# An encoder trunk's attention rebuilt: projections as Strassen groups summed in PSUM, heads' work in slots between products

## The chip, the core and the metric

One core of a Trainium2 chip runs the whole program. The metric is the device time of one execution in microseconds (us). Engines are named as the profile names them: PE is TensorE (matrix products and transposes), PEld its weight loads, DVE the vector engine, ACT the scalar engine, POOL the GpSimd engine, SP the engine that issues the DMA transfers of this kernel. PSUM is the memory into which PE writes its results, eight banks of 512 fp32 numbers in each of 128 partitions; SBUF is the working memory of all engines.

## What is computed

Two layers over a sequence of 1,024 rows of width 1,024. Layer 0 is attention with two families of heads, layer 1 a gated recurrence; each layer ends with a SwiGLU block, and every block is wrapped in two RMS norms. Everything is fp32. The change touches the attention of layer 0:

```python
def attention_mixer(h, w_in, rel_bias, w_out):
    proj = h @ w_in                       # 1024 x 3072
    part_a, part_b = proj[..., :3 * A_W], proj[..., 3 * A_W:]
    qa, ka, va = [t.reshape(b, s, 8, 64) for t in jnp.split(part_a, 3, axis=-1)]
    qs, ks, vs = [t.reshape(b, s, 8, 64) for t in jnp.split(part_b, 3, axis=-1)]
    out_a = chunked_relpos_attention(qa, ka, va, rel_bias)
    out_b = stick_breaking_attention(qs, ks, vs)
    return jnp.concatenate([out_a, out_b], axis=-1) @ w_out

# A, per head: softmax(q k^T / 8 + bias[clipped distance]) v over the own chunk of 64 rows and the 8 before it
# B, per head and block of 128 queries, z = q k^T / 8, keys strictly before the query:
        log_beta = jax.nn.log_sigmoid(z)
        log_1m_beta = jnp.where(causal, jax.nn.log_sigmoid(-z), 0.0)
        after = lax.cumsum(log_1m_beta, axis=3, reverse=True) - log_1m_beta
        w = jnp.where(causal, jnp.exp(log_beta + after), 0.0)
        o = einsum('bhqk,bkhd->bqhd', w, v)
```

A weight of a B head is thus the difference of two neighbouring products of (1 - sigmoid), taken from the query backwards.

## The kernel before

**Precision.** A big product of fp32 operands is made of three matmuls: each operand is split into hi, a copy rounded to the type fp32r, and lo, the rest, and hi·hi, hi·lo and lo·hi are summed in PSUM. `split` (L136 load, L143 hi on ACT, L144 lo on DVE) does this for 128x1024 numbers of weights, in a pool "main" that is open for the whole program (three raw buffers, eight for hi and lo). Transposes and the value products are plain fp32 matmuls.

**Hidden.** `pre_norm` makes the normalized rows of a tile of 128 (L164 squares on ACT, L167 and L168 POOL, L191 scaling on DVE), transposes them in eight 128x128 blocks on PE (L197), and `HiddenT.take` writes hi (L57, ACT) and lo (L58, DVE) of the transposed hidden hT.

**Heads.** Sixteen heads are taken in pairs: pairs 0 to 3 are A heads, 4 to 7 B heads, in the order 4, 5, 6, 7, 0, 1, 2, 3. For two pairs at a time the values are projected (L248 to L250, 24 matmuls of 256 columns for a tile of 128 rows and 4 heads), and copied out of PSUM by DVE (L253). `project` computes q and k of a pair, transposed (`proj_T`, L154 to L156, 512 columns), and lays for each head three operands: qs holds hi of q in 64 partitions and lo in the other 64, k1 and k2 hold hi and lo of k twice. A block of scores is then two matmuls 128 deep for each head and up to 512 keys:

```python
nc.tensor.matmul(sc, q, k1[:, ks], start=True, stop=False)
nc.tensor.matmul(sc, q, k2[:, ks], start=False, stop=True)
```

(L321, L322). `attend` goes over the eight tiles of 128 queries of a pair. An A head takes up to five blocks of 128 keys: bias and minimum on DVE (L325, L332), exponential with its sum on ACT (L333), division on DVE and POOL (L335, L336). A B head takes all blocks up to its own: sigmoid on ACT (L329), the mask on POOL (L338), a running product over the keys on DVE (L341), and the difference of neighbours (L344, DVE). Then for each four blocks of 128x128, PE transposes the weights (L354), ACT or DVE copies them to SBUF (L358, L360), and PE multiplies them with the values (L363: head 0 in the left 64 columns of the array, head 1 in the right). After four tiles ACT copies the output (L369) and SP stores it to DRAM (L370).

**Order.** The code names no order of engines. The framework's scheduler, with a timeline of its own, moves instructions past each other where their data and buffers allow it: the projections of the next pair (L154 to L156, L248 to L250) stand between the scores, transposes and values of the present one, and the loads and splits of the output weights (`out_product`, first load raw_5617) stand ahead of the last pairs' work. PSUM holds two banks for projections, one for outputs, three for scores, two for transposes.

After the attention, `out_product` loads the heads' outputs back (L415) and multiplies them by the output weights (L422 and following), with the pairs in the order of their making.

Of the kernel before, what the change touches and what calls it, by code (L numbers as in the profile page):

```python
# [8 lines left out]
F32 = mybir.dt.float32  # L9
F32R = mybir.dt.float32r  # L10
# [5 lines left out]
P = 128  # L16
# [8 lines left out]
BIG = 1e30  # L25

# [71 lines left out]

class Trunk:
# [4 lines left out]
    def __init__(self, ctx, tc, io):  # L104
# [3 lines left out]
        self.main = ctx.enter_context(tc.tile_pool(name="main", bufs=1))  # L108
# [113 lines left out]
    def attention(self, x_src, w_in, bias_t, o_dst, hT):  # L222
        nc, tc = self.nc, self.tc
        with ExitStack() as ctx:
            ap = ctx.enter_context(tc.tile_pool(name="att", bufs=1, reuse_waits="tile"))
            prp = ctx.enter_context(tc.tile_pool(name="attproj", bufs=1, space=PSUM, reuse_waits="tile"))
            pp = ctx.enter_context(tc.tile_pool(name="attp", bufs=1, space=PSUM, reuse_waits="tile"))

            def w_cols(c0, n):
                return w_in[:, c0:c0 + n].rearrange("(k p) c -> p k c", p=P)  # L230

            vbase = [1024, 1280, 2560, 2816]

            def v_weights(grp):
                wv = w_cols(vbase[grp], 256)
                return [self.split(wv[:, 4 * j:4 * j + 4, :], 4, 256) for j in range(2)]

            def v_tile(grp, w, vt, t2):
                ps = prp.tile([P, 512], F32, tag="proj", bufs=2, name=self.uid("psv"))
                for tt in range(2):  # L240
                    t = 2 * t2 + tt
                    hh, hl = hT.half[t // 4]
                    tok = slice((t % 4) * P, (t % 4) * P + P)
                    o = ps[:, tt * 256:(tt + 1) * 256]
                    for kt in range(KT):
                        wh, wl = w[kt // 4]
                        k4 = kt % 4
                        nc.tensor.matmul(o, hh[:, kt, tok], wh[:, k4, :], start=kt == 0, stop=False)  # L248
                        nc.tensor.matmul(o, hh[:, kt, tok], wl[:, k4, :], start=False, stop=False)
                        nc.tensor.matmul(o, hl[:, kt, tok], wh[:, k4, :], start=False, stop=kt == KT - 1)  # L250
                psv = ps.rearrange("p (a h b) -> p a h b", a=2, h=2)
                for h in range(2):
                    nc.vector.tensor_copy(vt[h][:, 2 * t2:2 * t2 + 2, :], psv[:, :, h, :])  # L253

            def v_alloc():
                return [ap.tile([P, NT, P], F32, tag="v", bufs=3, name=self.uid("v")) for _ in range(2)]

            def project(p):
                qb, kb = (p * P, 512 + p * P) if p < 4 else (1536 + (p - 4) * P, 2048 + (p - 4) * P)
                st = [[ap.tile([P, S], F32R, tag="st", bufs=12, name=self.uid("st"))  # L260
                       for _ in range(3)] for _ in range(2)]
                for which, c0 in ((0, qb), (1, kb)):
                    w = self.split(w_cols(c0, P), KT, P)
                    for half in range(2):
                        ps = prp.tile([P, 512], F32, tag="proj", bufs=2, name=self.uid("psq"))
                        self.proj_T(ps, w, slice(0, P), hT, half)
                        cs = slice(half * HALF, (half + 1) * HALF)
                        for h in range(2):
                            own, oth = (slice(0, 64), slice(64, P)) if h == 0 else (slice(64, P), slice(0, 64))
                            qs, k1, k2 = st[h]  # L270
# [675 lines left out]
```

## Time and profile before

| | before |
|---|---|
| median of 3 runs | 2258.68 us (2257.41 to 2261.26) |
| the profiled execution | 2262.01 us |
| its span | 2260.2 us |
| mean granted clock of PE | 0.993 |
| instructions | 30583 |
| PE busy in the span | 2201.2 us, 97% |
| PE's first transpose of the attention (L197) | 7.8 us |
| PE's first matmul of the output product (L422) | 518.46 us |

The profile is of one execution, and its own time stands beside its span in the table. In its rows an operation is written by engine, line, the names of what it writes and reads (out<-in), and its shape as partitions x elements. "busy" is time in which an engine executes; a wait is the idle time ahead of an instruction, put down to the one that released it. Matmuls overlap, so their price is better read from the distance of their starts than from their durations.

### The profile page before, as it was taken

The page shows a single profiled execution, that of the slowest core. Times are in us where ns is not written, and L with a number is a line of the kernel's source. Part 1 is how long each engine was busy: PE and PEld are TensorE (multiplying, and loading weights), DVE is VectorE, ACT ScalarE, POOL GpSimd, SP SyncE. Part 2 cuts the span into 40 slices and gives each one's busy share as a digit, 9 for nine tenths or more (in the row PEclk, how much of TensorE's full clock was granted, in tenths as well). Part 3 has the DMA queues.
Part 4 walks back from the last instruction along what each step waited for, and adds up shares of the span by engine and source line. Part 5 has one row for each costly group of instructions (what it writes and reads, how often), then busy time and mean ns, then how long its engine had stood idle before and what let it go on. Part 6 is the DMA issues. An engine that isn't in the chain of part 4 may idle for free. (4 is left out here: it accounts for less than half of the span.)

```text
span 2260.2 us, 30583 instructions
## 1 busy us (share of the span) xinstructions
PE 2201.2 (97%) x11136; PEld 1802.0 (80%) x11136; DVE 1551.9 (69%) x2514; ACT 1149.1 (51%) x2132; POOL 168.3 (7%) x370
## 2 busy tenths in 40 slices
PE   7999999999999999999999999999999999999997
PEld 6887888877678888888887777887788888888875
DVE  5676765464677767675866787536777767668665
ACT  4544455464665454532446567527755444424443
POOL 2111212131100000000001100001100000000010
PEclk9999999999999999999999999999999999999998
DMA  4101011124623333334558511358233333327466
GB/s 161 52 20 52 20 48 41 59 97 132 230 83 104 114 115 108 102 118 175 187 148 251 155 56 41 94 175 269 76 125 108 100 115 104 107 98 274 126 205 196
DMA packets 187271, 273.63 MB, mean 121 GB/s; under 512 B 13936, under 2 KB 115312, under 8 KB 187120
## 3 DMA queue, kind: packets, MB, share of 16 engines
q1 hardware_dynamic: 186480, 269.58, 38.0%
q10 hardware_dynamic: 640, 2.10, 0.3%
q8 instruction: 87, 1.43, 0.3%
q14 instruction: 64, 0.52, 0.1%
HBM read 206.09 MB, written 65.54 MB: 120 GB/s over the span
## 5 line engine op out<-in xcount | busy, mean ns | idle before, releaser
L509 PE MATMUL ps<-hS,q 128*128 128x512 f32 (+1 forms) x1288 | 490.9, 382 | 3.1 <-ACT hS L95 3.1
L510 PE MATMUL ps<-hS,q 128*128 128x512 f32 (+1 forms) x1288 | 490.9, 381 | 0.0
L511 PE MATMUL ps<-hS,q 128*128 128x512 f32 (+1 forms) x1288 | 489.9, 381 | 0.0
L490 DVE TENSOR_TENSOR q<-raw,q 128x512 fp32r<-128x512 f32 x308 | 204.7, 686 | 179.2 <-ACT q L489 178.7
L509 PEld LDWEIGHTS ps<-hS,q 128*128 128x128 f32 x1288 | 243.3, 189 | 50.2 <-ACT hS L95 3.9
L510 PEld LDWEIGHTS ps<-hS,q 128*128 128x128 f32 x1288 | 243.9, 189 | 46.7 <-DVE hS L88 0.4
L511 PEld LDWEIGHTS ps<-hS,q 128*128 128x128 f32 x1288 | 244.0, 189 | 45.8
L489 ACT CAST q<-raw 128x512 fp32r<-128x512 f32 x308 | 177.8, 616 | 168.8 <-DVE raw L498 130.4
L590 PE MATMUL ps<-o,o 128*128 128x512 f32 x616 | 240.9, 392 | 0.9 <-DVE o L585 0.8
L591 PE MATMUL ps<-o,o 128*128 128x512 f32 x616 | 238.2, 391 | 0.7 <-DVE o L701 0.7
L589 PE MATMUL ps<-o,o 128*128 128x512 f32 x616 | 221.1, 393 | 9.0 <-ACT o L700 5.5
L584 ACT CAST o<-raw 128x512 fp32r<-128x512 f32 x206 | 123.6, 620 | 193.8 <-PE ps L591 56.0
L478 ACT ACTIVATE raw<-raw,gcol 128x256 f32<-128x256 f32 x352 | 150.2, 498 | 139.0 <-DMA raw<-in_ffn_w_up_dram 71.8
L585 DVE TENSOR_TENSOR o<-raw,o 128x512 fp32r<-128x512 f32 x206 | 137.9, 688 | 66.4 <-ACT o L584 65.6
L589 PEld LDWEIGHTS ps<-o,o 128*128 128x128 f32 x616 | 115.7, 188 | 37.2 <-ACT o L700 7.7
L144 DVE TENSOR_TENSOR wlo<-raw,whi 128x1024 fp32r<-128x1024 f32 x76 | 93.4, 1230 | 66.0 <-ACT whi L143 65.1
L590 PEld LDWEIGHTS ps<-o,o 128*128 128x128 f32 x616 | 116.2, 189 | 26.6 <-DVE o L585 2.9
L591 PEld LDWEIGHTS ps<-o,o 128*128 128x128 f32 x616 | 116.1, 188 | 25.5 <-DVE o L701 1.6
L167 POOL TENSOR_SCALAR rs<-ss 128x1 f32<-128x1 f32 x64 | 31.8, 496 | 1270.2 <-ACT junk L164 1171.0
L143 ACT CAST whi<-raw 128x1024 fp32r<-128x1024 f32 x76 | 79.8, 1052 | 58.5 <-PE ps L155 24.7
L358 ACT COPY pt<-tr 128x512 f32<-128x512 f32 (+1 forms) x128 | 65.5, 527 | 78.5 <-PE tr L354 78.0
L154 PE MATMUL psq<-hT,whi 128*128 128x512 f32 x256 | 101.2, 395 | 1.1 <-DVE v L253 1.1
(185 smaller groups left out, 4237.6 us busy)
## 6 DMA issues: line engine op xcount, KB each, us to landing
raw<-in_ffn_w_down_dram SPq DMA_DIRECT2D x96, 256.0 KB, 4.6
raw<-in_ffn_w_gate_dram SPq DMA_DIRECT2D x44, 512.0 KB, 4.1
raw<-in_ffn_w_up_dram SPq DMA_DIRECT2D x44, 512.0 KB, 4.1
gS<-c SPq DMA_DIRECT2D x88, 256.0 KB, 3.6
raw<-gS SPq DMA_DIRECT2D x88, 256.0 KB, 3.0
gA<-c SPq DMA_DIRECT2D x66, 256.0 KB, 3.4
raw<-in_attn_w_in_dram SPq DMA_DIRECT2D x24, 512.0 KB, 3.9
raw<-in_attn_w_out_dram SPq DMA_DIRECT2D x24, 512.0 KB, 4.3
```

The source lines that it names most:

```text
L154: nc.tensor.matmul(ps, wh[:, kt, cols], hh[:, kt, :], start=kt == 0, stop=False)
L478: nc.scalar.activation(raw[:, i], raw[:, i], AF.Copy, scale=gain[:, 4 * k + i:4 * k + i + 1])
L489: self.last = nc.scalar.copy(t[:, 0], src).ins
L490: nc.vector.tensor_tensor(t[:, 1], src, t[:, 0].bitcast(F32), op=ALU.subtract)
L509: nc.tensor.matmul(ps, a[:, 0, kt, :], bh, start=kt == 0, stop=False)
L510: nc.tensor.matmul(ps, a[:, 0, kt, :], bl, start=False, stop=False)
L511: nc.tensor.matmul(ps, a[:, 1, kt, :], bh, start=False, stop=kt == 3)
L584: nc.scalar.copy(t[:, 0], src)
L585: tt(t[:, 1], src, t[:, 0].bitcast(F32), op=ALU.subtract)
L589: nc.tensor.matmul(ps, a[0], b[:, 0], start=first, stop=False)
L590: nc.tensor.matmul(ps, a[0], b[:, 1], start=False, stop=False)
L591: nc.tensor.matmul(ps, a[1], b[:, 0], start=False, stop=last)
```

## The change

The attention is written anew, and what surrounds it is adapted. Behind the attention the program stays as it was, with two exceptions: the order of pairs in the output product is 0 to 7, and the pool "main" is opened when the attention's pools have been closed, where before it was open from the start.

**Hidden in quadrants.** `HiddenH` holds the hidden as seven operands of a Strassen-Winograd product with hi and lo, in three tiles b0, b1, b2: the two halves of the sequence by the two halves of the width are four blocks, and the seven are these and their sums and differences. Tiles of rows come in the order 0, 4, 1, 5, 2, 6, 3, 7, so that a tile and the one 512 rows behind it can be combined. Behind each tile's transposes the A heads' values are projected from the same operands (24 matmuls of 512 columns) and stored to DRAM.

**Groups and products.** The other 2,560 columns (q and k of eight pairs, the B heads' values) are ten groups of 256 columns. A group is seven products, each 12 matmuls of 512 columns (three for each of four blocks of 128 of the contraction), where the direct way takes eight. Sums of products that share a term go on in the same PSUM bank (`first=False`); the others are added by ACT and DVE as they leave it. q and k go to DRAM and are loaded back for each pair. Values of B heads are differenced along the sequence, transposed back by PE, and stored, so that the running products are used as they are and L344's difference of weights is not made; one column of values is added with the output.

**Scores** are plain fp32 matmuls 64 deep: head 0 in partitions 0 to 63, head 1 in 64 to 127, into two PSUM banks that the next instructions read together. `turn` transposes up to 8 blocks into a double bank, which ACT copies to one buffer pt; the value matmuls of a tile come at the next slot, by `flush`.

**Order.** Each PE job is chained behind the one before (`run`, by issue_after). A slot is the scores of one tile with the transposes of the tile before it, or one of the two where both double banks are needed for one of them. After each product a credit grows by 1.35, up to 2.7; a slot costs 1, and is taken if the groups that its pair needs were ended three products ago. What is left when the products are through follows without any between. PSUM now holds two banks x, one yz, one for outputs, and two double banks "ct" that scores and transposes share.

```diff
+class HiddenH:
+    def take(self, t, ps, pool):
...
+        if t < 4:
+            f = self.f[t] = new("f", 2)
+            for q in range(2):
+                split(b0[0][:, q, :, cols], b0[1][:, q, :, cols], ps[q])
+                cast(f[:, q], ps[q])
+            return lambda z, kt: b0[z][:, kt // 4, kt % 4, cols]
+        b12, b22 = ps
+        f, e = self.f[t - 4], new("e", 1)
+        own = pool.tile([P, 2, 4, P], F32R, tag="own", bufs=1, name=self.uid("own"))
+        cast(e[:, 1], b12)
+        sub(f[:, 0], b12, f[:, 0])
+        split(own[:, 0], own[:, 1], b12)
+        split(b1[0][:, 0, :, cols], b1[1][:, 0, :, cols], b22)
+        sub(e[:, 1], b22, e[:, 1])
+        sub(e[:, 0], b22, f[:, 0])
+        sub(f[:, 1], f[:, 1], e[:, 0])
+        for src, i in ((e, slice(1, 3)), (f, slice(0, 4, 3))):
+            split(b2[0][:, i, :, cols], b2[1][:, i, :, cols], src)
...
-    def attention(self, x_src, w_in, bias_t, o_dst, hT):
+    def attention(self, x_src, w_in, w_v, bias_t, o_dst):
...
+            def run(jobs):
+
+                with tc.issue_after(state["after"]) if state["after"] else nullcontext():
+                    for job in jobs:
+                        state["after"] = job().ins
...
+            order = [0, 1, 2, 3, 8, 4, 5, 9, 6, 7]
...
+            def product(ps, i, first):
...
+                for kt in range(4):
+                    bh, bl = hS.op(i, 0, kt, FULL), hS.op(i, 1, kt, FULL)
+                    for x, y in ((a[:, 0, kt, :], bh), (a[:, 0, kt, :], bl), (a[:, 1, kt, :], bh)):
+                        jobs.append(lambda x=x, y=y, s=first and not jobs, e=kt == 3 and x is not y: nc.tensor.matmul(
+                            ps, x, y, start=s, stop=e, skip_group_check=True))
+                run(jobs)
...
+            def group(g):
...
+                x = bank("x", 2)
+                product(x, 0, True)
+                s1 = tmp()
+                nc.scalar.activation(s1, x, AF.Copy, scale=scale)
+                yield
...
+                product(x, 4, False)
+                u2 = tmp()
+                nc.scalar.copy(u2, x)
+                yield
...
+            def scores(p, i):
...
+                    held["k"] = cp.tile([P, S], F32, tag="k", bufs=1, name=self.uid("k"))
+                    nc.sync.dma_start(held["k"], qk[p][1])
...
+                if i % 4 == 0:
+                    held["q"] = cp.tile([P, 512], F32, tag="q", bufs=1, name=self.uid("q"))
...
+                sc = [pair_bank()[:, :, :w] for _ in range(n_c)]
+                run([lambda c=c, h=h: nc.tensor.matmul(
+                    sc[c][:, h], q[rows[h], i % 4 * P:i % 4 * P + P], k[rows[h], k0 * P + c * w:k0 * P + c * w + w],
+                    start=True, stop=True) for c in range(n_c) for h in range(2)])
...
+            for g in order:
+                for _ in group(g):
+                    unit += 1
+                    credit = min(credit + 1.35, 2.7)
+                    while credit >= 1 and at < len(slots):
+                        p = slots[at][0]
+                        need = [p] if p < 4 else [p, 8 + (p - 4) // 2]
+                        if not all(x in ready and ready[x] + 3 <= unit for x in need):
+                            break
+                        slot()
+                        at += 1
+                        credit -= 1
...
+            while at < len(slots):
+                slot()
+                at += 1
+            flush()
...
+            (nc.scalar.copy if n % 2 else nc.vector.tensor_copy)(vb, o)
...
-        with pool("h0", "right") as hp:
-            self.attention(x, io["attn_w_in"], io["bias_t"], oT, HiddenT(self, hp))
+        self.attention(x, io["attn_w_in"], io["attn_w_v"], io["bias_t"], oT)
+        self.main = ctx.enter_context(tc.tile_pool(name="main", bufs=1, reuse_waits="tile"))
...
-                                 hS, [4, 5, 6, 7, 0, 1, 2, 3])
+                                 hS, list(range(KT)))
```

**The instructions at three places.** Rows give line, operation, out<-in, shape, and xN where N of them follow each other. Lines are those of each kernel's own text; the changed text is longer, so that equal code has a higher line.

First, DVE at the start, where the hidden is made. Before, a tile costs two subtractions of hT, and the copies of values (v) stand among them:

```order
L58 TENSOR_TENSOR hT_100<-pst_244,hT_99 128x4x128
L253 COPY v_112<-psv_186 128x256
L253 COPY v_113<-psv_186 128x256
L58 TENSOR_TENSOR hT_100<-pst_249,hT_99 128x4x128
L144 TENSOR_TENSOR wlo_589<-raw_586,whi_588 128x1024
L58 TENSOR_TENSOR hT_100<-pst_265,hT_99 128x4x128
```

In the change (ct is the double bank that the transposes wrote, hS, own, e and f are hidden operands, x the rows, vb the values of a tile whose 24 matmuls PE has to end first):

```order
L615 SCALAR_TENSOR_TENSOR x_391<-x_391,rs_394,g_135 128x1024
L125 TENSOR_TENSOR hS_129<-e_237,hS_128 128x8x128
L125 TENSOR_TENSOR hS_129<-f_185,hS_128 128x2x4x128
L626 COPY vb_281<-ps_304 128x512
L125 TENSOR_TENSOR f_297<-ct_340,f_297 128x512
L615 SCALAR_TENSOR_TENSOR x_443<-x_443,rs_446,g_135 128x1024
L125 TENSOR_TENSOR hS_125<-ct_400,hS_124 128x4x128
L125 TENSOR_TENSOR own_350<-ct_340,own_350 128x512
```

The subtractions of the next pair of tiles (ct_340, ct_400), which their value matmuls need, now stand behind the copy vb_281.

Second, PE in the middle. Before, with pairs 4 and 5, the scheduler mixes values, transposes, scores (st) and projections of 256 columns one by one:

```order
L249 MATMUL psv_1705<-wlo_1649,hT_99 128x256
L250 MATMUL psv_1705<-whi_1648,hT_100 128x256
L363 MATMUL pso_808<-pt_1054,v_112 64x128 x4
L354 MATMUL tr_1243<-ident,pr_1221 128x128
L354 MATMUL tr_1243<-ident,pr_1232 128x128
L321 MATMUL sc_1295<-st_1082,st_1081 128x384
L322 MATMUL sc_1295<-st_1083,st_1081 128x384
L363 MATMUL pso_808<-pt_1065,v_112 64x128 x4
```

In the change, with the first tiles of pair 0, two slots stand between two products:

```order
L358 MATMUL ps_883<-hS_128,q_739 128x512
L516 MATMUL ps_901<-pt_878,v_899 64x128 x2
L459 MATMUL ct_907<-k_832,q_844 128x384 x2
L499 MATMUL ct_923<-ident,pr_862 128x128 x4
L516 MATMUL ps_901<-pt_922,v_899 64x128 x4
L459 MATMUL ct_935<-k_832,q_844 128x512 x2
L499 MATMUL ct_951<-ident,pr_906 128x128 x6
L358 MATMUL ps_775<-hS_128,q_755 128x512
```

The values from pt_922 stand next behind the scores that follow the transposes ct_923, whose copy pt_922 is; no product lies between.

Third, the end of the attention. Before, on SP, the output weights (raw) stand among and ahead of the last stores of the attention (L370):

```order
L136 DMA raw_5797<-in_attn_w_out_dram 128x1024
L289 DMA bias_5191<-in_bias_t_dram 128x640
L415 DMA act_5735<-oT_73 128x384
L415 DMA act_5765<-oT_74 128x384
L415 DMA act_5795<-oT_75 128x384
L370 DMA oT_75<-ob_5041 128x512
L370 DMA oT_76<-ob_5335 128x512
L370 DMA oT_76<-ob_5583 128x512
```

In the change the first of these weights comes behind the last store (L524):

```order
L510 DMA v_4288<-vn_121 128x1024
L524 DMA oT_76<-ob_4116 128x512
L455 DMA q_4343<-qk_0_116 128x512
L524 DMA oT_77<-ob_4291 128x512
L524 DMA oT_77<-ob_4410 128x512
L189 DMA raw_4587<-in_attn_w_out_dram 128x1024
```

On PE the change ends the attention with the last two tiles of pair 7, no product between them, and the output product (L650) follows:

```order
L459 MATMUL ct_4467<-k_4259,q_4343 128x512 x2
L459 MATMUL ct_4468<-k_4259,q_4343 128x512 x2
L499 MATMUL ct_4481<-ident,pr_4422 128x128 x6
L499 MATMUL ct_4489<-ident,pr_4422 128x128 x8
L516 MATMUL ps_4409<-pt_4480,v_4288 64x128 x14
L499 MATMUL ct_4515<-ident,pr_4466 128x128 x8
L499 MATMUL ct_4525<-ident,pr_4466 128x128 x8
L516 MATMUL ps_4409<-pt_4514,v_4288 64x128 x16
L650 MATMUL ps_4579<-whi_4589,ah_4593 128x512
```

Before, these rows were blocks of four transposes and four values each, as in the second place, with the first matmul of the output product (L422) right behind the last of them.

More of the change, by code (lines that the diff above doesn't have):

```diff
@@ L25 @@
 BIG = 1e30
+FULL = slice(0, 512)
 def rows(t, x):
@@ new lines, in attention @@
+            hS = HiddenH(self, hp)
+            with self.pool("rows") as sp:
+                self.rows_in(ap, sp, x_src, w_v, va, hS, bank, pair_bank, operand)
+            cp = ctx.enter_context(self.pool("core"))
+            state = {"after": None}
+            def run(jobs):
[3 more added lines that the diff above has]
+            order = [0, 1, 2, 3, 8, 4, 5, 9, 6, 7]
```

426 lines of the change are left out of this document (264 added, 162 removed).

## Prediction

> **What bounds the kernel now.** I read the page first, then the busy time by stage, then what TensorE (PE) itself waited for in the stage that the change touches.
>
> ```profile
> span 2260.2 us, 30583 instructions
> PE 2201.2 (97%) x11136; PEld 1802.0 (80%) x11136; DVE 1551.9 (69%) x2514; ACT 1149.1 (51%) x2132; POOL 168.3 (7%) x370
> 7.80:60.00 52.20, 43.62 (x283) 40.93 (x284) 30.77 (x38) 23.85 (x38) 14.11 (x20) 0.93 0.45 148
> 60.00:480.00 420.00, 420.00 (x2973) 350.51 (x2972) 271.25 (x490) 212.48 (x428) 70.30 (x186) 1.00 0.13 40
> 480.00:518.50 38.50, 35.28 (x316) 25.32 (x314) 24.88 (x96) 25.76 (x62) 15.34 (x25) 1.00 0.34 116
> ```
>
> The last three lines are stretches of the span: length, then busy time (instructions) of PE, PEld, DVE, ACT and POOL, granted clock, DMA. The attention is the stretch from PE's first transpose at 7.8 to 518.5 us, where its last value matmul hands over to the output product. In its middle PE is busy without a gap for 420 us while DVE is busy 65% and ACT 51%. The next view, PE's own waits up to 520 us, says the same (waited for, total us, times, longest).
>
> ```profile
> PE pst L197 <- DVE h L191: 7.8, 1, 7.8
> PE psv L250 <- DVE hT L58: 3.5, 2, 2.9
> PE pst L197 <- DVE hT L58: 2.6, 1, 2.6
> PE pso L363 <- ACT pt L358: 2.3, 3, 1.4
> PE psv L248 <- ACT hT L57: 1.5, 2, 1.2
> PE psq L154 <- DVE v L253: 1.1, 1, 1.1
> PE sc L321 <- DVE mn L325: 0.8, 1, 0.8
> ```
>
> After the start, PE waited 11.8 us (the last six lines). So of 518.5 - 7.8 = 510.7 us, **499 us are PE work**. The old order is as full as an order can be: the change can gain only by giving PE less to do, and everything it leaves uncovered is new.
>
> **PE work after the change.** The busy time of a matmul overlaps the next one's, so prices are taken from starts in PE's timeline (start, busy, line, tiles, count).
>
> ```profile
> 168.16 0.39 PE L322 MATMUL sc<-st,st 128*128 128x512 f32 x1
> 168.39 0.39 PE L155 MATMUL psq<-hT,whi 128*128 128x512 f32 x1
> 168.71 0.44 PE L363 MATMUL pso<-pt,v 128*64 128x128 f32 x4
> 169.08 0.66 PE L354 MATMUL tr<-ident,pr 128*128 128x128 f32 x4
> 169.66 0.66 PE L363 MATMUL pso<-pt,v 128*64 128x128 f32 x8
> 170.25 0.66 PE L354 MATMUL tr<-ident,pr 128*128 128x128 f32 x4
> 170.66 0.48 PE L321 MATMUL sc<-st,st 128*128 128x512 f32 x1
> ...
> 172.60 0.39 PE L154 MATMUL psq<-hT,whi 128*128 128x512 f32 x1
> ...
> 174.18 0.39 PE L155 MATMUL psq<-hT,whi 128*128 128x512 f32 x1
> 601.15 1.04 PE L197 MATMUL pst<-ident,mg 128*128 128x128 f32 x8
> 602.03 9.61 PE L422 MATMUL ps<-raw,act 128*128 128x512 f32 x22
> 611.47 1.04 PE L197 MATMUL pst<-ident,mg 128*128 128x128 f32 x8
> ```
>
> Seven 512-column fp32r matmuls from 172.60 to 174.18: 0.227 us each. Eight transposes from 601.15 to 602.03: 0.109. Plain f32, 128x512: 22 records in 9.44 us, two records a matmul, so 0.858 us, or 0.2145 per 128 columns. Value matmuls are f32 with the two heads in the two column halves: 4 records take 0.37, 8 take 0.59, so 0.2185 per block pair (one key block, both heads) and 0.15 per batch. One head alone would cost 0.2145 at the f32 price, so the two halves run side by side. Entering a value batch costs another 0.09 (168.39 to 168.71 is 0.32 where a matmul takes 0.227): 0.25 a batch in all. A transposing batch costs about 0.06 beyond its transposes.
>
> Counted in the new program: 192 value-projection and 70 x 12 = 840 product matmuls, 1032 x 0.227 = 234.3; transposes 64 + 528 + 32 new ones for the B heads' values, 624 x 0.109 = 68.0; values 264 block pairs x 0.2185 = 57.7, in 64 batches x 0.25 = 16; some 70 transposing batches x 0.06 = 4.
>
> The scores are the unknown: instead of two fp32r passes over a stacked 128-deep operand (4 x 0.227 per 512 columns and pair) they are f32 matmuls 64 deep, head 0 in the upper half of the array's rows and head 1 in the lower, into two banks. No row of this trace uses row halves. Bounds: side by side as the value matmuls are, 264 x 0.2145 = 56.6 us; one after the other, twice that, 113. I take 56.6, because the nearest row (L363, two halves of the other kind) shows overlap, plus 0.25 a batch as there (16; bounds 0 and 22).
>
> The Trainium skill's page "TensorE: Matmul & The Clock Gate" (Part 3, Packing small matmuls) states that tiles in different row groups run concurrently, with 3.07 times for four of them. By that factor the pair would be estimated at 57 to 74 us, so the sum would be at most 17 us worse; the trace agrees for column halves and no run so far shows it for row halves.
>
> Sum: 234.3 + 68.0 + 57.7 + 16 + 4 + 56.6 + 16 = **453 us, 46 less than the 499**.
>
> **What is no longer covered.** PE's order is now written out, so each wait is read from the order against these durations (two lines of the timeline; then line, engine, shape, count | busy, mean ns; then DMAs with KB and us to landing).
>
> ```profile
> 6.50 1.28 DVE L191 SCALAR_TENSOR_TENSOR h<-x,rs,g 128x1024 f32<-128x1024 f32 x1 [5.62 <-POOL rs L168]
> 518.46 0.50 PE L422 MATMUL ps<-whi,ah 128*128 128x512 f32 x1
> L191 DVE SCALAR_TENSOR_TENSOR h<-x,rs,g 128x1024 f32<-128x1024 f32 x8 | 10.7, 1341 | 9.2 <-POOL rs L168 9.0
> L58 DVE TENSOR_TENSOR hT<-pst,hT 128x512 fp32r<-128x512 f32 x16 | 10.9, 687 | 12.9 <-ACT hT L57 12.9
> L325 DVE CUSTOM_DVE_ANT_0 pr<-sc,bias 128x320 f32<-128x320 f32 x64 | 28.7, 487 | 7.2 <-PE sc L322 6.4 <-PE tr L354 0.3
> L333 ACT ACTIVATE pr<-pr,mn 128x640 f32<-128x640 f32 x32 | 26.4, 827 | 19.4 <-DVE mn L332 19.1 <-DVE sm L335 0.2
> L336 POOL TENSOR_SCALAR pr<-pr,sm 128x640 f32<-128x640 f32 x32 | 25.8, 810 | 63.4 <-DVE sm L335 55.2 <-PE psq L156 4.9 <-PE sc L322 1.4
> L338 POOL TENSOR_SCALAR_AFFINE_SELECT pr<-pr 128x128 f32<-128x128 f32 x64 | 28.8, 454 | 133.9 <-ACT pr L329 133.0 <-issue 0.4
> L341 DVE TENSOR_TENSOR_SCAN pr<-pr,zero 128x1024 f32<-128x1024 f32 x8 | 18.3, 2288 | 4.0 <-POOL pr L338 4.0
> L329 ACT ACTIVATE pr<-sc 128x512 f32<-128x512 f32 x24 | 14.1, 607 | 14.8 <-PE tr L354 13.2 <-PE sc L322 1.5
> L358 ACT COPY pt<-tr 128x512 f32<-128x512 f32 x92 | 52.6, 588 | 63.1 <-PE tr L354 62.7
> L143 ACT CAST whi<-raw 128x1024 fp32r<-128x1024 f32 x28 | 29.3, 1053 | 29.4 <-PE psq L155 15.4 <-issue 7.2 <-PE psv L249 3.9
> raw<-in_attn_w_out_dram SPq DMA_DIRECT2D x24, 512.0 KB, 4.3
> raw<-gS SPq DMA_DIRECT2D x88, 256.0 KB, 3.0
> ```
>
> *Start.* The first products need all hidden groups, so only the A heads' value matmuls stand beside the making of the hidden. In the order DVE's copy of one tile's values stands ahead of the next tiles' evacuations, so PE and DVE take turns. Three pairs of tiles each cost 48 x 0.227 = 10.9 on PE, 16 transposes (1.7), and then on DVE the gain (1.34) and three 512-column subtractions (2.1) before PE has work again: 16 us. Tile 0 ends near 21 us (DVE's first 14 instructions, 4 x 1.34 + 10 x 0.69 = 12.3, from 6.50), the pairs near 69, the last tile near 76. Of these 68 us after PE's first transpose 192 x 0.227 + 64 x 0.109 = 50.6 are PE's work and about 2 the first product's: **16 us of waiting and of the start's lower clock** (bounds 5 and 22). The old start had 8.7 of the 11.8.
>
> *Middle.* 70 products of 2.72 us with slots between. I compared, tile by tile, PE's work between a tile's scores and its transposes with the chain between them: for five band blocks 4 x 0.49 + 2 x (0.83 + 0.19) + 0.81 and hand-overs, 5.6 us; for eight stick-breaking blocks the last sigmoid (1.0 for 1,024 columns, estimated from the 0.61 for 512), the mask over both heads (0.45 to 0.9, I take 0.75), two scans of 2.29 and hand-overs, 6.9 us. Most tiles have 8 to 13 us of PE work there and wait for nothing. Ten, mostly the first of a pair, are short, by 13 us together. At 14 places the values follow their transposes with no product between: PE waits for ACT's copy (0.59 and up, 0.7 with hand-over), and where the next tile's two exponentials stand ahead of that copy on ACT, 2.2; nine and five of these, 17. Six transposing batches follow at once on scores that hold both double banks, 0.9 each, 5. The half of q for tiles 4 to 7 has one buffer and comes from DRAM: twice only 1.6 us of PE work covers its 3 us load and issue, and three loads of v are short by 0.6: 7. Sum 42; a wait often shortens the next, so I take **40** (bounds 5 and 60).
>
> *Tail.* The last pairs become ready with the last products, so behind the last product stand 14 tiles' values, 13 tiles' transposes and 12 tiles' scores, 50 us of PE work by the prices above, with nothing between. Worked through for tile 5 of the last pair, scores, sigmoids, scans, transposes, copies and values give a period of 6.0 where PE works 4.9; for two blocks 3.0 against 1.9; after the last scores PE needs 3.4 and the chain takes 10.9. Summed, 74: **24 us of waiting**.
>
> *Hand-over.* Before, the output weights were loaded and split during the tail (L422 starts at 518.46, right behind the last values). Now their first load stands behind the last store of the output on SP, since the main pool takes the attention's memory: last output copy some 0.3 (a quarter of the columns of L358's 0.59), load 4.3, cast 1.05 and hand-overs, **6.6 us with PE idle**.
>
> ```profile
> 627.10:633.90 6.80, 3.88 (x32) 3.44 (x30) 6.80 (x15) 4.34 (x7) 1.28 (x3) 1.00 0.23 92
> 633.90:640.70 6.80, 5.37 (x24) 5.15 (x24) 4.86 (x11) 3.89 (x7) 0.00 (x0) 0.50 0.00 1
> ```
>
> A stretch with PE 57% busy was followed by 6.8 us at half the granted clock (the second last but two number). An idle of 6.6 us will do the same: up to 3.4 us lost, I take **3**.
>
> Waiting after: 16 + 40 + 24 + 6.6 + 3 = 90, against 11.8. Change: -46 + 78 = **+32 us**. The rest (the 1741.7 us behind 518.5) is the same code and taken as unchanged. The profiled execution took 2262.0 us, 3.3 over the median, so 2294 there and **2290 us** as a median (2294.0 - 3.3, rounded).
>
> **Rivals.**
> 1. *The scores' row halves don't overlap.* Against: the column halves do. For: no row shows it. Then 57 more, 2347.
> 2. *The products cover the middle.* The mechanism is the slot order: nearly all chains there have more PE work beside them than they last, and each wait lets the other engines catch up. If the middle's 40 fall below 10, the change gains or breaks even; at none it is 2250, **faster**. For: ACT and DVE have about 60% to do there by my count. Against: the immediate follow-ons stand in the order and cannot move.
> 3. *The clock.* In the tail PE works 50 of 74 us, in the start 51 of 68, near the 57% that preceded the half-clock stretch. If half the tail's eleven stretches of 6.8 us fall to it at some 3 us each, and two in the start, 23 more: 2313. The Trainium skill's page "TensorE: Matmul & The Clock Gate" (HAM oscillation) has this as a rule, the clock halving after one idle window of about 3.4 us and oscillating where PE idles between bursts. By that rule this rival's time is the likelier one; the trace shows both halving (after 57% above) and no halving at 480 to 518.5 us, where the clock stayed 1.00.
>
> That the program doesn't do what it says is excluded by the order.
>
> **How the numbers follow.** Chances: my forecast 0.53 (2266 to 2312, from the bounds of start, batches and middle), rival 1 0.15, rival 2 0.22, rival 3 0.10. Range 2246 to 2350: rival 2 at its floor, rival 1 with a little of the rest; under one in five is left out. A measurement of this kernel tells about 0.2% (4.5 us) from no change. Faster: most of rival 2 (0.16) and 0.02 of the forecast, 0.18. Same: 0.05 and 0.04, 0.09. Slower: 0.73.
>
> **What would show it.** PE's stretch from first transpose to last value matmul should end near 540 us. Right or wrong by step: the start of two scores on row halves within some 0.01 us of each other and 0.86 us per 512 columns; the last value-projection matmul near 76; PE's waits on ACT's copies, POOL and the scans 30 to 50 us in the middle; 70 to 78 us from the last product to the last value; 6 to 7 us of idle after it. The forecast is wrong if the middle shows PE as full as before, or if scores take 1.7 us per 512 columns.

## The result, and the profile after

The changed kernel takes 2295.4 us (median of 4, 2292.66 to 2301.13) against 2258.81 for the kernel before in the same comparison: a ratio of 1.0164, 95% interval 1.0140 to 1.0188. The forecast was 2290. The profiled execution took 2293.06 us. Its page begins with

```profile
span 2291.1 us, 29480 instructions
PE 2188.6 (96%) x10664; PEld 1742.6 (76%) x10664; DVE 1515.3 (66%) x2458; ACT 1164.3 (51%) x2125; POOL 145.4 (6%) x278
```

The span is 30.9 us longer although PE is busy 12.6 us less. Where that lies is seen in the busy time by stretch. The stretches are the start (first transpose to last value projection), the middle (to the last product), the tail (to the last value matmul), the hand-over, and the rest (columns as before: length, then PE, PEld, DVE, ACT, POOL, clock, DMA):

```profile
8.00:74.60 66.60, 59.44 (x258) 47.58 (x259) 47.28 (x63) 37.92 (x64) 5.97 (x14) 0.95 0.32 117
74.60:465.10 390.50, 362.79 (x2351) 267.99 (x2350) 199.78 (x472) 196.58 (x395) 66.17 (x112) 0.99 0.28 94
465.10:540.60 75.50, 60.06 (x489) 38.82 (x488) 38.85 (x30) 39.55 (x58) 4.90 (x12) 0.89 0.24 78
540.60:546.40 5.80, 0.05 (x2) 0.00 (x0) 0.01 (x1) 1.41 (x2) 0.00 (x0) 0.87 0.79 255
546.40:2291.10 1744.70, 1706.26 (x7568) 1388.20 (x7568) 1228.00 (x1892) 886.16 (x1604) 66.89 (x132) 0.99 0.45 140
```

The output product starts at 546.4 where it started at 518.46: 27.9 us. The rest took 1744.7 against 1741.7: 3.0. That is the whole difference of the two spans (the medians lie 36.6 apart, since the profiled execution after the change is 2.3 us below its median and the one before is 3.2 above). PE's own waits up to 560 us (the second line is ahead of the first transpose):

```profile
PE ps L516 <- ACT pt L502: 14.7, 23, 1.7
PE ct L618 <- DVE x L615: 8.0, 1, 8.0
PE ps L623 <- ACT own L128: 6.3, 4, 2.0
PE ct L499 <- DVE pr L469: 6.3, 4, 2.3
PE ps L650 <- ACT whi L196: 5.8, 1, 5.8
PE ct L499 <- POOL pr L487: 4.8, 3, 4.3
PE ct L422 <- DVE o L420: 4.2, 2, 3.2
PE ct L499 <- ACT pr L464: 3.8, 8, 1.6
PE ct L499 <- DVE mn L477: 2.9, 4, 0.9
```

Before, 11.8 us of waits stood here, all causes counted; now the lines above but the second hold 48.8 of 53.9, and no single one dominates. Some rows of PE's timeline carry the prices:

```profile
99.65 2.88 PE L358 MATMUL ps<-hS,q 128*128 128x512 f32 x12
...
109.58 5.42 PE L358 MATMUL ps<-hS,q 128*128 128x512 f32 x12
...
445.37 3.00 PE L358 MATMUL ps<-hS,q 128*128 128x512 f32 x12
448.30 1.97 PE L516 MATMUL ps<-pt,v 128*64 128x128 f32 x32
...
522.78 1.77 PE L459 MATMUL ct<-k,q 64*128 64x448 f32 x8
...
538.64 2.01 PE L516 MATMUL ps<-pt,v 128*64 128x128 f32 x32 [0.28 <-ACT pt L502]
546.41 2.07 PE L650 MATMUL ps<-whi,ah 128*128 128x512 f32 x4 [5.76 <-ACT whi L196]
```

Three things are to be seen. Seven blocks of scores for both heads take 1.77 us (the forecast's 7 x 0.2145 + 0.25 is 1.75): the row halves run side by side. From a product to the values behind it are 448.30 - 445.37 = 2.93 us where twelve matmuls cost 2.72. And one product, after the first tile's wait of 4.3 us on POOL, took 5.42 us instead of 2.88: it ran at half the clock, as the stretch around it shows (the second last but two number).

```profile
108.00:114.80 6.80, 5.82 (x14) 4.09 (x14) 1.23 (x5) 0.93 (x4) 2.31 (x4) 0.50 0.00 0
```

### The profile page after: what moved, and what is told of

It reads as the page before. It is cut to its first block, busy times and chain, and to the rows that moved or that the text cites. A ratio compares the mean times of both kernels' runs of the same rounds, so it can differ in the third digit from the quotient of the medians.

```text
span 2291.1 us, 29480 instructions
## 1 busy us (share of the span) xinstructions
PE 2188.6 (96%) x10664; PEld 1742.6 (76%) x10664; DVE 1515.3 (66%) x2458; ACT 1164.3 (51%) x2125; POOL 145.4 (6%) x278
## 5 line engine op out<-in xcount | busy, mean ns | idle before, releaser
L737 PEld LDWEIGHTS ps<-hS,q 128*128 128x128 f32 x1288 | 243.4, 190 | 50.3 <-ACT hS L96 4.0
L738 PEld LDWEIGHTS ps<-hS,q 128*128 128x128 f32 x1288 | 243.9, 189 | 46.7 <-DVE hS L89 0.5
L739 PEld LDWEIGHTS ps<-hS,q 128*128 128x128 f32 x1288 | 243.9, 189 | 45.7
L358 PE MATMUL ps<-hS,q 128*128 128x512 f32 x840 | 212.3, 404 | 0.7 <-ACT s L401 0.7
L358 PEld LDWEIGHTS ps<-hS,q 128*128 128x128 f32 x840 | 156.0, 192 | 41.6 <-issue 7.9
L469 DVE TENSOR_TENSOR_SCAN pr<-pr,zero 128x128 f32<-128x128 f32 (+7 forms) x64 | 83.5, 1349 | 74.4 <-POOL pr L465 72.3
L220 POOL TENSOR_SCALAR rs<-ss 128x1 f32<-128x1 f32 x64 | 25.9, 405 | 1302.2 <-ACT junk L217 1170.1
L208 PE MATMUL ps<-hT,whi 128*128 128x512 f32 x256 | 99.8, 390 | 1.2 <-DVE hT L59 1.2
```

The costliest lines, as they stand in the source:

```text
L358: jobs.append(lambda x=x, y=y, s=first and not jobs, e=kt == 3 and x is not y: nc.tensor.matmul(ps, x, y, start=s, stop=e, skip_group_chec ...
L737: nc.tensor.matmul(ps, a[:, 0, kt, :], bh, start=kt == 0, stop=False)
L738: nc.tensor.matmul(ps, a[:, 0, kt, :], bl, start=False, stop=False)
L739: nc.tensor.matmul(ps, a[:, 1, kt, :], bh, start=False, stop=kt == 3)
```

## The experiments

The stretches of all kernels, from the starts in PE's timeline, in us (time: median; where a ratio is given below, of several rounds, otherwise of one run):

| kernel | start | middle | tail | hand-over | time |
|---|---|---|---|---|---|
| the change | 66.4 | 390.5 | 75.5 | 6.0 | 2295.4 |
| e1_no_chain | 65.3 | 371.0 | 65.4 | 6.5 | 2266.5 |
| e2_main_early | 66.8 | 390.8 | 78.7 | 0.2 | 2289.6 |
| e3_value_copies_late | 58.1 | 391.0 | 75.5 | 6.2 | 2289.0 |
| e4_heads_apart | 65.1 | 397.4 | 85.9 | 6.2 | 2310.8 |
| e5_half_slots | 66.9 | 376.1 | 71.6 | 6.2 | 2273.2 |
| e6_four_edits | 58.0 | 371.7 | 74.6 | 0.2 | 2257.8 |
| e7_output_in_tail | 57.9 | 370.1 | 73.7 | 0.2 | 2259.5 |
| e8_psum_given_back | 58.4 | 372.8 | 73.5 | 0.2 | 2258.6 |
| e9_more_slots | 58.1 | 379.1 | 68.1 | 0.2 | 2257.0 |
| e10_band_pairs_last | 58.0 | 367.0 | 97.6 | 0.2 | 2279.5 |
| e11_psum_back_later | 57.9 | 369.4 | 74.1 | 0.2 | 2249.4 |
| e12_with_more_slots | 58.8 | 377.9 | 68.6 | 0.2 | 2251.9 |

### No chain between scores and transposes

```diff
-                if p >= 4:
-                    for c in range(n_c):
-                        nc.scalar.activation(pr[:, :, c * w:c * w + w], sc[c], AF.Sigmoid)
...
-                        tr[:, (j - a) * P:(j - a + 1) * P], pr[:, h, (kb - k0) * P:(kb - k0 + 1) * P], self.ident)
+                        tr[:, (j - a) * P:(j - a + 1) * P], self.ident, self.ident)
```

> Left out: bias, minimum, exponential, division, sigmoid, mask and scan, that is all work between a tile's scores and its transposes, which turn the identity instead; scores, transposes, ACT's copies and value matmuls stay in number, size and PE order. Theory (waits on those chains and on the copies fill the middle and the tail): PE's waits there, 25 us in the middle and 15 in the tail by the waits view, fall to 15 or less together, the stretch from the last product to the last value from 75.4 to 54-62 us, and the one from the first transpose to the last value from 532.6 to 495-512. Rival (PE's own work or a lowered clock fills that time): less than 10 us in all, and the tail stays above 68.

Middle and tail, by stretch:

```profile
73.10:444.10 371.00, 357.34 (x2351) 266.31 (x2350) 96.06 (x142) 130.48 (x235) 9.05 (x28) 1.00 0.30 99
444.10:509.60 65.50, 56.45 (x490) 38.08 (x488) 2.92 (x5) 23.62 (x38) 0.00 (x0) 0.90 0.27 90
```

The middle lost 19.5 us and the tail 10.1, 29.6 together; the last value comes 501.7 us after the first transpose, inside the theory's 495 to 512. The tail at 65.4 is above its 54 to 62: its clock is still 0.90, so that a part of the tail's length isn't the chains'. PE's waits in the two fell from 41 to 21 us, not to 15. Those on ACT's copies are 13.3 of the 21:

```profile
PE ps L488 <- ACT pt L474: 13.3, 24, 1.4
```

With nothing between, the values of a tile wait for the copy of its own transposes, although ACT is busy only 24 of the tail's 65.5 us. Another 6.4 of the 21 are waits on two loads (k and v).

### Output weights early

```diff
+            hctx.close()
+            self.main = self.ctx.enter_context(tc.tile_pool(name="main", bufs=1, side="right", reuse_waits="tile"))
             while at < len(slots):
```

> The pool of the output weights is opened in the memory of the hidden operands once the last product is emitted, so that loads and splits stand among the tail. Theory (the hand-over costs 5.8 us of idle PE and some 3 of lowered clock behind it): the output product starts within 0.5 us of the last value, and the time is 2286 to 2290, 6 to 9 less. Rival (ACT's and DVE's 14 casts and subtractions, about 15 us, get between the chains of the tail and give it back): the tail grows from 75.4 to over 80 and the time stays within 3 us of 2295.

The end of the attention, and the tail by stretch:

```profile
542.76 1.85 PE L517 MATMUL ps<-pt,v 128*64 128x128 f32 x30
544.54 0.50 PE L653 MATMUL ps<-whi,ah 128*128 128x512 f32 x1
```

```profile
465.60:544.40 78.80, 59.37 (x490) 39.12 (x489) 43.60 (x34) 43.08 (x62) 5.23 (x12) 0.91 0.35 122
```

The hand-over is gone (0.2 us), and the time is 2289.6 (ratio to before 1.0137, 1.0122 to 1.0152), inside the 2286 to 2290 expected but only 5.8 less. The interval overlaps that of the change (1.0140 to 1.0188): the closed gap is shown by the trace, the gain in time by itself is not clear of noise. About half of the rival is there too: DVE and ACT have 4.8 and 3.5 us more in the tail, which grew by 3.2.

### Value copies late

```diff
+                with self.tc.issue_after(need[1 - n % 2]) if need else nullcontext():
+                    (nc.scalar.copy if n % 2 else nc.vector.tensor_copy)(vb, o)
-            (nc.scalar.copy if n % 2 else nc.vector.tensor_copy)(vb, o)
```

> At the start a tile's copy of values stands behind the next tile's casts and subtractions that its value matmuls need, on ACT and on DVE. Theory (PE and DVE take turns since the copy stands ahead): the stretch from the first transpose to the last value-projection matmul falls from 66.6 to 59-62 us, and the time by 4 to 7. Rival (DVE's own 47 us with its latencies bound the start): it stays above 65, and the time is unchanged.

```profile
7.80:66.00 58.20, 55.02 (x256) 44.19 (x257) 47.87 (x64) 38.83 (x65) 6.73 (x15) 1.00 0.41 140
```

The start fell by 8.3 us, more than expected, and the time by 6.4 to 2289.0 (ratio 1.0140, 1.0123 to 1.0156). DVE has the same 47 us of work; only the place of each tile's copy in its queue (DVE's and ACT's in turn) changed. The clock of the start rose from 0.95 to 1.00 with it. As with the output weights, the stage shows it better than the time, whose interval reaches that of the change.

### Heads apart

```diff
-                    start=True, stop=True) for c in range(n_c) for h in range(2)])
+                    start=True, stop=True) for h in range(2) for c in range(n_c)])
```

> Where a tile has two score chunks, the four matmuls are issued as head 0, head 0, head 1, head 1 instead of alternating. If row halves run side by side only when they are issued next to each other, one of the two overlaps is lost in 32 tiles of 184 key blocks in all: 184 x 0.2145 / 2 = 20 us more PE work, of which some fills waits: 10 to 20 us later at the last value. If each half has its own queue: the starts of head 0 and head 1 stay together, and nothing changes.

One batch of the same tile, timelines of the change and then of this kernel (PE and ACT):

```profile
424.86 1.77 PE L459 MATMUL ct<-k,q 64*128 64x448 f32 x8
...
425.98 1.73 ACT L464 ACTIVATE pr<-ct 128x896 f32<-128x896 f32 x2 [0.58 <-PE ct L459]
```

```profile
430.00 1.78 PE L459 MATMUL ct<-k,q 64*128 64x448 f32 x8
...
431.87 1.73 ACT L464 ACTIVATE pr<-ct 128x896 f32<-128x896 f32 x2 [1.34 <-PE ct L459]
```

The first expectation's 10 to 20 us came true (the last value is 16.0 us later), but not by its cause, and the second's "nothing changes" missed. PE's price did not change (1.78 against 1.77), so the halves ran side by side though issued apart; yet the kernel got slower, middle and tail by 17.3 us. What moved is the chain: ACT's first sigmoid starts 1.87 us after the batch instead of 1.12, since it needs head 1's first chunk, now the third matmul of four. That is 0.75 us for 448 columns (a band tile of 320 columns shows 0.53: DVE's first minimum starts 1.50 us after its batch instead of 0.97); over the 32 tiles with two chunks (16 band tiles of 320 columns, and four each of 320, 384, 448 and 512) 19.7 us. So a delay in the chain costs time although PE's work is as it was. That the sum comes near the 17.3 is luck: of the 19.7 some 14 belong to the middle, which grew by 6.9 only, and 5.6 to the eight such tiles of the tail, which grew by 10.4, and the clock fell with it:

```profile
470.60:556.50 85.90, 63.59 (x490) 42.59 (x488) 38.89 (x30) 39.71 (x58) 4.88 (x12) 0.86 0.21 69
```

### Slots at half products

```diff
-                run(jobs)
+                run(jobs[:6])
+                tick()
+                run(jobs[6:])
...
+                credit = min(credit + 0.675, 2.7)
```

> Slots may stand in the middle of a product too: the credit grows by 0.675 after each 6 matmuls, and at most one slot is taken there, so that 6 matmuls (1.4 us) stand between any two slots of the middle. Theory (the middle waits because slots follow each other at once): PE's waits in the middle, 25 us by the waits view, fall to 8-14, among them those on ACT's copies from 8.4 to under 3, and the time by 10 to 16, to 2280-2286. Rival (each further entry into a product costs PE 0.1 us, some 40 of them, and what is waited for only moves): waits fall by less than 5, and the time by under 4. Start and tail as they are.

```profile
74.80:450.90 376.10, 362.72 (x2372) 268.14 (x2371) 199.79 (x470) 196.31 (x395) 62.98 (x113) 0.99 0.29 98
450.90:522.50 71.60, 53.92 (x470) 35.23 (x468) 38.23 (x29) 37.62 (x55) 4.62 (x12) 0.95 0.25 82
```

PE's waits on ACT's copies in the middle of the change, and then the largest waits in the middle of this kernel, with those on ACT's copies last:

```profile
PE ps L516 <- ACT pt L502: 8.4, 13, 1.2
```

```profile
PE ct L424 <- DVE o L422: 4.5, 2, 3.5
PE ps L358 <- ACT s L403: 3.5, 3, 2.2
PE ct L501 <- POOL pr L489: 2.0, 2, 1.7
PE ps L518 <- ACT pt L504: 1.0, 1, 1.0
```

The middle lost 14.4 us. Its waits are 13.2 us instead of 26.1, those on ACT's copies 1.0 instead of 8.4. The time fell by 22, to 2273.2 (ratio 1.0062, 1.0042 to 1.0081), more than the 10 to 16 expected. The tail, which was to stay, lost 3.9: it has one batch of scores and one of values less (20 records), and its clock rose from 0.89 to 0.95.

### Four edits together

Output weights early, value copies late, slots at half products, and the transposes of the B heads' values one and two products behind their difference:

```diff
+                    done2()
                     for d in state["done"]:
                         done(*d)
```

Here done2 transposes, copies and stores the values of one pair whose difference done has made.

> Together: output weights early, value copies late, slots at half products, and the transposes of the B heads' values one and two products behind their difference (PE waits 4.2 us on that difference). If the four are independent: 3 to 6, 6, 10 to 16 and 4 us less, 2263 to 2272, still above the kernel before (2258). Rival (what one removes the next wait takes): 2273 or more.

2257.8, a ratio of 0.9993 (0.9984 to 1.0003): below the expected range, level with the kernel before. Taken from 2295.4, the three gains measured singly (5.8, 6.4 and 22.2) and the 4 expected of the fourth, which was not run by itself, give 2257.0: the edits add up.

### Output product in the tail, and three kernels on what it did

```diff
+                if state["values"] is not None:
+                    run([jobs.pop(0) for _ in range(fill.get(n_v, 0))])
+                    n_v += 1
                 slot()
```

Here fill says how many matmuls of the output product stand ahead of which batch of values. Their three PSUM banks live on behind the attention, so the later stages take their six banks in a fixed turn out of two pools.

> As the one with four edits, and 36 matmuls of the output product (four of its eight blocks, for three PSUM banks that the products have left) stand in the tail, 3 or 6 of them ahead of ten batches of values. Theory (PE waits there for chains on other engines, and falls to half clock since it idles): the 8.2 us of matmuls lie in the waits, and the windows of half clock shrink: the last value comes at most 3 us later than in that kernel, and the time falls by 5 to 10, to 2254-2266. Rival (the other engines' chains themselves wait for PE in the tail): the tail grows by about 8 and nothing is gained.

In the attention the theory held: with 36 matmuls more in it the tail is 73.7 against 74.6 (clock 0.95 against 0.89, one profile each), and the matmuls that follow (matched by their number from the program's end) ran 7 to 8 us ahead through the first SwiGLU. But the time is 2259.5 (1.0006, 0.9997 to 1.0015), not 5 to 10 less. The lead was lost in the recurrence, where PE waits 11.3 us in this kernel and 3.9 in the one before it:

```profile
PE ps L1096 <- DVE xc L1071: 11.3, 3, 8.7
```

```diff
             self.ectx.close()
+            pctx.close()
+            self.pp = ctx.enter_context(tc.tile_pool(name="pp1", bufs=1, space=PSUM, reuse_waits="tile"))
...
             gO = ffn(0, hS)
```

> As the kernel with the output product in the tail, whose matmuls run 7 to 8 us ahead of the kernel with four edits up to some 1310 us of the span, and lose it by 1550 us, in the layers that this study does not touch. Theory: the loss comes from the six PSUM banks of the later stages, which there were taken in a fixed turn out of two pools; here both pools are closed behind the output product, and one pool of eight banks is opened as before. Expected: the lead of 7 to 8 us is kept to the end, 2248 to 2252. Rival (the later stages lose it for another reason): 2256 to 2261 as before.

2258.6 (0.9995, 0.9986 to 1.0004), the rival's number. The recurrence's wait fell to 4.2, as the theory of the fixed turn has it, but the lead was now lost right behind the output product: with the pools closed there, the scheduler set the last tiles' transposes with no matmuls of the next layer between:

```profile
PE pst L253 <- ACT mg L245: 8.5, 1, 8.5
PE pst L253 <- ACT mg L85: 5.0, 2, 4.7
```

The last kernel has these two added lines behind `gO = ffn(0, hS)` instead.

> As the kernel with the output product in the tail, whose lead of 7 to 8 us was kept through the output product and the first SwiGLU half and lost in the recurrence; the two PSUM pools are closed and one opened behind that first half, where no normalization of a last tile waits (closed behind the output product, in the other kernel, the transposes of the last tiles stood alone on PE for 17 us). PE's order from the second half of that SwiGLU on is then that of the kernel with four edits. Theory: the lead stays to the end, 2248 to 2253, under the kernel before (2259) by 0.3 to 0.5%. Rival: the boundary of the two halves costs it, 2255 or more.

The lead stayed: **2249.4 us, a ratio of 0.9959 (0.9946 to 0.9971)**, 0.4% under the kernel before and faster than the change. Its page and stretches:

```profile
span 2246.0 us, 29466 instructions
PE 2171.8 (97%) x10664; PEld 1732.9 (77%) x10664; DVE 1515.4 (67%) x2458; ACT 1163.0 (52%) x2125; POOL 140.5 (6%) x278
```

```profile
8.00:65.90 57.90, 55.53 (x256) 44.79 (x257) 47.91 (x64) 38.60 (x65) 6.58 (x15) 1.00 0.39 139
65.90:436.00 370.10, 359.86 (x2380) 265.87 (x2379) 200.99 (x472) 196.91 (x397) 62.65 (x113) 1.00 0.29 99
436.00:510.00 74.00, 60.88 (x502) 41.64 (x501) 42.21 (x33) 41.42 (x60) 4.83 (x11) 0.95 0.37 132
```

### Rate of slots, and band pairs last

```diff
-                credit = min(credit + 0.675, 2.7)
+                credit = min(credit + 0.8, 2.7)
```

> As the kernel with PSUM given back, with a credit of 0.8 instead of 0.675 after each 6 matmuls, so that the middle takes slots faster and fewer are left behind the last product (11 batches of values against 13). Theory (a slot left for the tail costs its uncovered chain, some 1 us each): 2 to 4 us less. Rival (the slots run into pairs that are not ready, long runs of products follow, and the denser slots wait more): same or up to 5 us more.

2257.0 (0.9984, 0.9975 to 0.9993): the tail lost 5.4 us and the middle gained 6.3, as the rival had it. The time is 1.6 under that of e8, between the rival's "same" and the theory's 2 to 4, and the two intervals overlap: not decided.

> The same with a credit of 0.8 instead of 0.675 after each 6 matmuls. Before, this moved 5.4 us from the tail to the middle and was within 2 us. Theory (the sum of uncovered chains is set by the pairs' readiness, not by the rate): within 3 us of the other kernel of this call. Rival (fewer slots in the tail keep the clock up): 3 to 5 us less.

2251.9 (0.9964, 0.9950 to 0.9977), 2.6 over e11: within 3, as the theory had it; the rival's 3 to 5 less is out. That the pairs' readiness sets the sum is not shown by this.

```diff
-            order = [0, 1, 2, 3, 8, 4, 5, 9, 6, 7]
+            order = [0, 4, 8, 5, 6, 9, 7, 1, 2, 3]
...
-            pairs = list(range(8))
+            pairs = [0, 4, 5, 6, 7, 1, 2, 3]
```

The credit is 0.75 here, and the matmuls of the output product take the pairs in the same order, 3 of them ahead of each of twelve batches of values.

> As the kernel with PSUM given back, with pairs in the order 0, 4, 5, 6, 7, 1, 2, 3 (groups accordingly, credit 0.75), so that band pairs stand in the tail: 5 blocks a tile at most instead of 8, chain 5.6 us against 6.9 with the scans. Theory (the tail is bound by a tile's chain, and B tiles have the longer one): although 16 batches of values are left instead of 13, the tail grows by no more than 5 us, and the time stays within 4 us. Rival (it is bound by the number of tiles, about 5 us each): the tail grows by 10 to 15 us.

```profile
432.80:530.50 97.70, 67.30 (x514) 43.48 (x513) 34.98 (x153) 47.70 (x112) 23.40 (x38) 0.88 0.34 118
```

```profile
PE ps L529 <- DMA v<-va: 9.5, 2, 8.7
```

2279.5 (1.0085, 1.0070 to 1.0101). The tail grew by 24.1 against e8, more than either expected. Of this 9 is a wait of another kind, the line above: a load of v, issued at 439.0 among the loads of the output weights, took 8.0 us to land (the other one took 4.6), and PE idled 8.7 us for it. The remaining 15 are the top of the rival's 10 to 15. The tail holds 17 batches of values (one more than was counted there) against 13; without that load PE idles 1.2 us for each, in e8 1.0. So shorter chains did not make up for more tiles. How the tail would do without the late load was not run.

## Why the prediction was right

**The sum and its stages.** 2290 was forecast and 2295.4 measured. The stages below are those of the profiled execution, 2293.06 us, for which 2294 stood; the median lies 2.3 above it where the forecast put it 3.3 below (and 2294.0 less 3.3 is 2290.7). By stages: the start 68 and measured 66.4; the attention's end near 540, and the last value matmul started at 540.4; the tail 74 and 75.5; the hand-over 6.6 and 6.0; 3 for the clock behind it, and the rest took 3.0 more, of which the clock shows 2.7 (half speed up to 551.7, the second last but two number, 5.3 us behind the start of the output product):

```profile
544.90:551.70 6.80, 5.29 (x13) 4.13 (x14) 3.68 (x3) 3.59 (x4) 0.00 (x0) 0.50 0.71 237
```

The middle follows as 390 and was 390.5. How 2266 to 2312, the range of the forecast itself, follows from the bounds of its terms the working does not show.

**The scores**, the largest unknown, came out at the price taken (1.77 against 1.75), so rival 1 is out.

**The step that was mis-sized is the split between work and waits.** The forecast had 453 us of PE work and 80 of waiting ahead of the hand-over. Measured, PE is busy 59.4 + 362.8 + 60.1 = 482.3 and idle 7.2 + 27.7 + 15.4 = 50.3. Idle time is 30 us less than said, work 29 more, and the two errors cancel: that the sum came so near is luck. Summed from PE's timeline by kind (start to next start, less the idle time), the 1,032 fp32r matmuls took 257.0 us where 234.3 stood, the transposes 79.9 for 72.0, the scores 74.0 for 72.6 and the values 71.5 for 73.7. About half of the 29 is the clock: up to the last value six stretches, 34.1 us together, ran at half, with PE busy in 31, which makes 15.5 us of PE's busy time. The forecast's sum has the clock of the start only, under waiting. A product between a transposing and a value batch costs 2.93 - 2.72 - 0.09 = 0.12 more than counted, in some 60 places 7. About 7 are left open.

**Start.** The cause held: the copy's place in the queues was worth 8.3 us. Of the 16 us forecast 7.2 are idle; 3.4 of the rest are a clock of 0.95, which vanished with the waits.

**Middle.** The waits by cause were right in kind and too large: on ACT's copies 8.4 where 17 stood, on loads 1.3 where 7 stood, on the B values' difference 4.2, which wasn't listed. That half of them come from slots without enough of a product between is shown by moving only the slots: 26.1 us of waits became 13.2, and the middle lost 14.4. Rival 2's counter-argument (the follow-ons stand in the order) was right for this program; with the slots spread its covered middle nearly comes about (10.2 us idle in e11).

**Tail.** 24 us of waiting were forecast; 15.4 are idle and some 8 are clock (0.89). Rival 3 happened, then, but inside the term and not on top of it: what was counted as waiting for chains was two thirds waiting and one third matmuls at half speed.

**Hand-over.** Right in size, and removed by opening the pool earlier; the tail takes half of it back.

## What to carry to other kernels

Where an engine has been full, count what a new order leaves uncovered before counting the work that it saves: here the first outweighed the second by 31 us. When a written-out order has waits, look first for places where two dependent steps stand next to each other and spread the filler between them; moving slots by half a product was worth 22 us, the most of any single edit here. A gain in one stage is only a gain when the order behind it keeps it: the same 8 us were lost twice in other layers by the way PSUM was handed over.

## What the runs showed of the hardware that was not expected

Row halves overlap without being issued alternately: two matmuls of head 0 and then two of head 1 take 1.78 us, where one after the other would be some 3.3 (four of 448 columns at 0.2145 per 128 are 3.0, and 0.25). But what waits for the third of them seems to be released only when the second is through; that is read from ACT's start at 1.87 us, and not tested by itself.

Half clock follows short idling: after the first tile's wait of 4.3 us a whole product ran at 5.42 us, and in the tail, behind two waits of 1.0 and 1.4 us, a stretch with PE busy 84% still had it:

```profile
500.50:514.20 13.70, 11.56 (x50) 6.26 (x50) 4.15 (x4) 4.94 (x8) 0.82 (x2) 0.50 0.08 29
```

Ahead of each of the six half-clock stretches up to the last value PE had been idle for 1.7 us or more of the 3.4 before. But not every such wait does it: e11 has waits of 1.9 and 2.2 us in its middle, and the clock there is 1.00. PE's busy time at half clock looks like work; the clock column, or a longer distance from start to start, tells it from matmuls that are needed.

The Trainium skill's page "TensorE: Matmul & The Clock Gate" (HAM oscillation) describes such halving where PE idles longer than about 3.4 us between bursts. The wait of 4.3 us agrees with it; the other five stretches follow waits of 2.3 us at most, so here shorter ones did it too.
